# A depthwise conv as float32 products in column groups on TensorE, and the norms' sums and weight low parts off GpSimd

## The chip, the cores and the metric

One NeuronCore of a Trainium2 chip runs the whole program in one launch. The metric is the device time in microseconds (us) of the launch, median of several runs; smaller is better. TensorE multiplies a stationary tile (up to 128 x 128) with a moving one (up to 128 x 512) into PSUM; VectorE (DVE), ScalarE (ACT) and GpSimd (POOL) work elementwise; SyncE (SP) issues most DMAs.

## The reference

Two transformer blocks on 512 tokens of 1024 channels, float32. The first has a parallel mixer (conv branch and attention), cross attention to a memory of 256 tokens and a conv-gated feed-forward; the second has two layers of half-weighted SwiGLU around a pooling mixer and a latent attention (MLA). The change touches the mixer's conv branch and the norms:

```python
def rmsnorm(x, g):
    return x * lax.rsqrt(jnp.mean(x * x, axis=-1, keepdims=True) + EPS) * g

def parallel_mixer(h, ...):
    z = jnp.einsum("bsd,dc->bsc", h, w_in)           # 1024 -> 1792
    a_val, a_gate = z[..., :512], z[..., 512:1024]   # then q, k, v
    a = a_val * jax.nn.sigmoid(a_gate)
    a = dwconv_centred(a, conv_dw, conv_dw_b)        # 31 taps, each channel by itself
    a = jax.nn.silu(layernorm(a, conv_ln_g, conv_ln_b))
    ...
    return jnp.einsum("bsc,cd->bsd", jnp.concatenate([a, att], -1), w_out)

x = x + rmsnorm(parallel_mixer(rmsnorm(x, g1), ...), g2)     # block 1, and likewise
x = x + rmsnorm(memory_cross_attention(rmsnorm(x, g3), ...), g4)
x = x + rmsnorm(conv_gated_ffn(rmsnorm(x, g5), ...), g6)
```

## The kernel before

Activations lie transposed: 128 channels on the partitions, 512 tokens along the free dimension, so x is eight tiles `x0` to `x7`. Every float32 operand of a large product is split into two exact parts of a shorter format, hi (a cast on ScalarE) and lo (the rest, by a subtraction), and `mm3` (L165) makes three products of them: hi hi (L168), hi lo (L169) and lo hi (L170). Weights come through SP into `raw` (three buffers, 512 KB a unit, `fetch` L127); `cook` (L132) splits them, with the low part on VectorE or, for `wshare` of every four units, on GpSimd (`lo_on_pool`, L144). `linear` (L172) runs the products of one output tile after another into PSUM and calls an evacuation.

A tile framework places the instructions: it orders each engine's work by priority (place in the program) and by when operands and buffers are free by its own model, and sets the semaphores. On the chip each engine then runs its own list in order.

**Norms.** `sums` (L202) adds squares over the partitions: for each tile of squares four float32 products of 128 columns with a stationary tile of 32 columns of ones, one per block of 128 tokens, into PSUM partitions 0, 32, 64 and 96. The result is turned (`columns`), its reciprocal root found in eleven small VectorE operations (`newton`), and spread to rows by float32 products with the identity (`bcast_ps`). `gather` (L313) keeps the squares to two tiles: GpSimd adds all but the last. `pre` (L321) scales and splits x for the next stage and makes the squares; `post_collect` (L337) takes squares of a stage's output as it is evacuated; `settle` (L349), run by the next `pre`, multiplies the output's tiles by the rows (two on VectorE, six on GpSimd, L364) and adds them to x on VectorE (L369). Three stages end so: mixer, memory and conv_ffn. `warm` (L375) runs products that nobody reads while TensorE waits there.

**Mixer** (L561). `ORDER` runs the 14 output tiles of w_in: gate and value of four channel tiles, k, v and four q tiles. `ev_val` (L597) makes `at`, the gated channel tile, and queues `conv_taps` (L542): 31 taps, six of them on TensorE (`conv_pe`, three products each with diagonal matrices that GpSimd builds, L530), one on ScalarE, 24 on VectorE as multiply-and-add of a shifted `at` (L556). `step` interleaves them: six behind each w_in tile, 30 ahead of attention, eight a head. Attention runs eight heads, the scores one head ahead; two units of the memory's key and value projections (`mem_kv`, L464) follow each head. `conv_norm` (L737) runs in three steps at heads 3, 6 and 7. w_out takes attention's half first, then the conv's, into all eight PSUM buffers.

Of the kernel before, what the change touches and what calls it, by code (L numbers as in the profile page):

```python
# [26 lines left out]
# order of the taps' offsets: the even ones from the middle, then the odd ones  # L27
TAPS = sorted(range(-(KTAPS // 2), KTAPS // 2 + 1), key=lambda d: (d % 2, abs(d), d))
# [5 lines left out]
_VECS = [  # L34
    ("g_mix", 8), ("conv_w", 4 * KTAPS), ("conv_b", 4), ("cln_g", 4), ("cln_b", 4),
# [25 lines left out]
class Kern:  # L61
# [41 lines left out]
    # -- small access helpers --  # L103
# [7 lines left out]

    def t(self, tag="t", dt=F32, w=S, name="t"):
        return self.pools[tag].tile([P, w], dt, name=name, tag=tag)
# [43 lines left out]
    def load_tile(self, w, nt, nk):  # L157
        """Stationary tiles of output tile nt: list over k of (hi, lo) [P, P]."""
        res = []
        for k0 in range(0, nk, 8):  # L160
            n = min(8, nk - k0)
            res += self.tiles(self.load_unit(w[nt, :, k0 * P:(k0 + n) * P], n * P), n)
        return res

    def mm3(self, ps, w, x, start, stop):  # L165
        """ps += w.T @ x with w, x each given as exact (hi, lo) parts."""
        mm = self.nc.tensor.matmul
        mm(ps, w[0], x[0], start=start, stop=False)  # L168
        mm(ps, w[0], x[1], start=False, stop=False)  # L169
        self.mmi = mm(ps, w[1], x[0], start=False, stop=stop)  # L170
# [10 lines left out]
    # -- split an fp32 tile (SBUF or PSUM), optionally scaled per partition --  # L181
# [31 lines left out]
    def columns(self, sm, dim, eps=0.0, w=1):  # L213
        """sm / dim + eps in columns [P, block, w], in PSUM."""
# [8 lines left out]
    def newton(self, v, n):  # L223
        """rsqrt of v [P, n] on the vector engine."""
# [14 lines left out]
    def rstd(self, sqs, dim, nb=4):  # L239
        """rsqrt(mean + eps) in columns from squares [P, nb * P], summed over the list."""  # L240
        sm = self.sums([(self.c("ones"), sq) for sq in sqs], nb)
        v = self.columns(sm, dim, EPS)
        return self.newton(v.rearrange("p j r -> p (j r)"), nb)
# [24 lines left out]
    def bcast_ps(self, R, nb=4, w=1):  # L268
        """Columns to rows of all partitions (row r of w in its share of them), exact float32."""
# [14 lines left out]
    def expand(self, R, w, tag="t"):  # L284
        """Columns -> [32 * block + r, tokens], zero outside the block, as exact parts."""
# [13 lines left out]
    def spread(self, X, r, tag="mi"):  # L299
        """Row r of every block, on all partitions."""  # L300
# [6 lines left out]
    # -- residual stream --  # L307
# [5 lines left out]
    def gather(self, sqs, sq, last, w=S):  # L313
        """Sum of squares so far: at most two tiles, the last one kept apart."""
        if not sqs or last:
            return sqs + [sq]
        self.nc.gpsimd.tensor_tensor(out=sqs[0][:, :w], in0=sqs[0][:, :w], in1=sq[:, :w],  # L317
                                     op=ALU.add)
        return sqs

    def pre(self, gname, dve_squares=(), tag2="xs"):  # L321
        """Gain times x as exact parts, and the reciprocal rms in quadrant form."""
        xs, sqs = [], []
# [4 lines left out]
        for k in range(ND):  # L328
# [5 lines left out]
            sqs = self.gather(sqs, sq, k == ND - 1 or bool(dve_squares))  # L334
        return xs, self.rstd(sqs, D)

    def post_collect(self, gname, tag="xs"):  # L337
        """Evacuation of a stage's output that a norm follows; pre() of the next stage adds it."""
        st = self.pending = {"y": [], "sqs": []}

        def evac(nt, ps):
# [4 lines left out]
            st["sqs"] = self.gather(st["sqs"], sq, nt == ND - 1)  # L346
        return evac

    def settle(self):  # L349
        """Generator: adds the pending normed output to x, a tile a step."""  # L350
# [6 lines left out]
        R = self.rstd(st["sqs"], D)  # L357
# [15 lines left out]
    SETTLE = 2  # L373
# [32 lines left out]
    def rope(self, src, g, gs, cos, sin):  # L406
        """Rotary embedding along the partitions (pairs 16 apart), gains g, gs folded in."""
# [11 lines left out]
    def stack(self, src, r, tag, on_pool=False):  # L419
        """Exact parts of the 64 rows src[64 r:], one in each half of a tile."""  # L420
# [27 lines left out]
    def mem_prep(self):  # L448
        """Gain times memory as exact parts."""
# [14 lines left out]
    def mem_kv(self):  # L464
        """Generator: key and value projections of the memory, a weight unit a step."""
# [37 lines left out]
    NPE = 6  # L503
    PE_AT = 0
    CP_TAG = "pt"
    STEP_IN = 6
    KV_HEAD = 2
    STEP_PRE = 30
    STEP_HEAD = 8
    KT_TAG = "pr"  # L510
    PT_TAG = "t"
    CN_AT = (3, 6, 7)
    CN_AF = (0, 0, 1)
    ORDER = (0, 1, 8, 2, 3, 9, 4, 5, 10, 6, 7, 11, 12, 13)
    W_IN, W_KV, W_OUT, W_MEM = 4, 4, 0, 1

    def tap(self, n):
        """Output and input ranges of tap n."""
        d = TAPS[n]
        return (slice(0, S - d), slice(d, S)) if d >= 0 else (slice(-d, S), slice(0, S + d))  # L520

    def conv_pe(self, i, at):
        """The taps of channel tile i that run on PE, as products with diagonal matrices."""
        nc = self.nc
        ah, al = self.split(at, None, "cv", name="ah")
        ps = self.ps(self.CP_TAG, "cps")
        for n0 in range(0, self.NPE, 2):
            c = 2 * (i * KTAPS + n0)
            dg = self.t("pr", F32R, name="dg")
            nc.gpsimd.tensor_tensor(  # L530
                out=dg.rearrange("p (n t) -> p n t", n=4),
                in0=self.ident.unsqueeze(1).to_broadcast([P, 4, P]),
                in1=self.cws[:, c:c + 4].bitcast(F32).unsqueeze(2).to_broadcast([P, 4, P]),
                op=ALU.mult)
            for n in range(2):
                o, s = self.tap(n0 + n)
                hi, lo = dg[:, 2 * n * P:(2 * n + 1) * P], dg[:, (2 * n + 1) * P:(2 * n + 2) * P]
                self.mm3(ps[:, o], (hi, lo), (ah[:, s], al[:, s]), n0 + n == 0,
                         n0 + n == self.NPE - 1)
        return ps  # L540

    def conv_taps(self, i, at, acc):  # L542
        """Generator: the other taps of channel tile i, on DVE."""
        nc = self.nc
        w = lambda n: self.cwh[:, i * KTAPS + n:i * KTAPS + n + 1]
        first = KTAPS // 2
        o, sl = self.tap(first)
        nc.scalar.activation(acc[:, o], at[:, sl], AF.Identity, scale=w(first),  # L548
                             bias=self.v("conv_b", i))
        nc.gpsimd.tensor_copy(acc[:, :1], self.v("conv_b", i))  # L550
        ps = None
        for m, n in enumerate(n for n in range(self.NPE, KTAPS) if n != first):
            if m == self.PE_AT:
                ps = self.conv_pe(i, at)
            o, s = self.tap(n)
            nc.vector.scalar_tensor_tensor(out=acc[:, o], in0=at[:, s], scalar=w(n),  # L556
                                           in1=acc[:, o], op0=ALU.mult, op1=ALU.add)
            yield
        nc.vector.tensor_tensor(out=acc, in0=ps, in1=acc, op=ALU.add)

    def mixer(self):  # L561
        nc = self.nc
        a = self.a
        self.cwh = self.t("tb", name="cwh")[:, :4 * KTAPS]
        ws0 = {0: self.tiles(self.cook(self.raw0, UNIT, 4), 8)}
        xs, R1 = self.pre("g_mix", (1, 3, 5))
        nc.gpsimd.tensor_scalar(out=self.cwh, in0=self.v("conv_w", 0, 4 * KTAPS), scalar1=0.5,
                                scalar2=1.0, op0=ALU.mult, op1=ALU.mult)
        self.cws = self.t("tb", F32R, name="cws")[:, :8 * KTAPS]
# [823 lines left out]
```

## Time and profile before

| | us |
|---|---|
| median of three runs | 2589.59 (2588.21 to 2589.89) |
| span of the profiled execution | 2588.3 |
| TensorE products busy | 2496.1 (96%) |
| VectorE busy | 1385.5 (54%) |
| ScalarE busy | 919.1 (36%) |
| GpSimd busy | 521.8 (20%) |

The mixer lies at 0 to 321 us of the span, the memory's attention up to 460, the conv-gated feed-forward up to 842; the rest is block 2. A matmul's busy time includes its way through the array, so neighbours overlap, and the spacing of starts is the better measure of what one costs. The profile's clock column is the share of TensorE's full clock that was granted, a mean over a stretch; it has two levels, 2.4 GHz (1.00) and 1.2 GHz (0.50). Each float32 product shows as two instructions.

### The profile page before, as it was taken

What the parts mean: (1) busy time and instruction counts of PE and PEld (TensorE: products, weight loads), DVE (VectorE), ACT (ScalarE), POOL (GpSimd) and SP (SyncE); (2) the same over time, 40 slices, a digit from 0 to 9 for tenths busy, and PEclk for the clock granted to TensorE, in tenths of its full rate; (3) what the DMA queues carried; (4) which work ended last, traced back from release to release, by engine and by line L of the source; (5) the groups of instructions that cost most, each with busy time, mean ns of one, the idle gap of its engine ahead of it and who ended that gap; (6) DMA issues with size and microseconds to landing.
All of it is one profiled execution on the core that took longest, in us unless ns stands there. A gap on an engine that the chain in (4) does not pass through costs nothing.

```text
span 2588.3 us, 29365 instructions
## 1 busy us (share of the span) xinstructions
PE 2496.1 (96%) x11668; PEld 2037.2 (79%) x11668; DVE 1385.5 (54%) x1877; ACT 919.1 (36%) x1332; POOL 521.8 (20%) x417
## 2 busy tenths in 40 slices
PE   7879989899999899999999999999999999999999
PEld 6667768688888688888888888888887778888887
DVE  7997563686632645533655543555433576555522
ACT  3336534354422333322422322323222455422221
POOL 4575232311100311101211100111000144111100
PEclk9889999999999999999999999999999999999999
DMA  4211211133333222234232333223332210333232
GB/s 163 66 67 49 90 57 58 64 98 98 96 95 97 69 94 96 95 98 132 74 98 98 97 98 96 97 95 95 98 98 88 78 62 19 104 98 97 92 107 79
DMA packets 68201, 229.80 MB, mean 89 GB/s; under 512 B 7456, under 2 KB 9632, under 8 KB 68064
## 3 DMA queue, kind: packets, MB, share of 16 engines
q1 hardware_dynamic: 66688, 225.35, 27.1%
q0 software_dynamic: 1232, 2.36, 0.3%
q8 instruction: 91, 1.49, 0.2%
q14 instruction: 46, 0.38, 0.0%
q10 hardware_dynamic: 144, 0.23, 0.0%
HBM read 225.80 MB, written 2.10 MB: 88 GB/s over the span
## 4 chain that ended last, share of the span: by engine, by line
PE 86%; DVE 4%; ACT 1%; issue 0%; ACTq 0%
PE ps L169 26%; PE ps L168 26%; PE ps L170 26%; DVE x L369 1%; DVE xl L190 1%; PE wo L168 1%; PE wo L169 1%; PE wo L170 1%; PE pt L124 1%; PE po L169 0%; PE bc L274 0%; PE po L168 0%; PE po L170 0%; PE sc L168 0%; DVE wlo L140 0%
## 5 line engine op out<-in xcount | busy, mean ns | idle before, releaser
L138 ACT CAST whi<-raw 128x1024 fp32r<-128x1024 f32 (+2 forms) x432 | 440.5, 1021 | 1217.7 <-PE ps L169 767.5
L140 DVE TENSOR_TENSOR wlo<-raw,whi 128x1024 fp32r<-128x1024 f32 (+2 forms) x400 | 559.3, 1400 | 492.6 <-ACT whi L138 487.5
L169 PE MATMUL ps<-xl,whi 128*128 128x512 f32 x2008 | 789.8, 394 | 18.6 <-DVE xl L190 18.5
L168 PE MATMUL ps<-xh,whi 128*128 128x512 f32 x2008 | 784.9, 393 | 15.0 <-ACT xh L189 14.7
L170 PE MATMUL ps<-xh,wlo 128*128 128x512 f32 x2008 | 786.6, 392 | 0.0
L169 PEld LDWEIGHTS ps<-xl,whi 128*128 128x128 f32 x2008 | 380.5, 189 | 104.6 <-DVE xl L190 25.0
L168 PEld LDWEIGHTS ps<-xh,whi 128*128 128x128 f32 x2008 | 379.7, 189 | 97.3 <-ACT xh L189 16.2
L170 PEld LDWEIGHTS ps<-xh,wlo 128*128 128x128 f32 x2008 | 380.7, 190 | 79.8 <-issue 0.9
L168 PE MATMUL ps<-ah,whi 128*128 128x512 f32 x880 | 342.3, 389 | 0.0
L169 PE MATMUL ps<-al,whi 128*128 128x512 f32 x880 | 342.3, 389 | 0.0
L170 PE MATMUL ps<-ah,wlo 128*128 128x512 f32 x880 | 342.3, 389 | 0.0
L877 DVE TENSOR_TENSOR g<-ps,bct 128x512 f32<-128x512 f32 x176 | 120.6, 691 | 389.9 <-PE ps L170 382.8
L882 POOL TENSOR_TENSOR g<-g 128x512 f32<-128x512 f32 x88 | 119.0, 1353 | 856.5 <-ACT whi L138 457.6
L317 POOL TENSOR_TENSOR sq<-sq 128x512 f32<-128x512 f32 x72 | 112.7, 1566 | 535.8 <-ACT sq L310 533.9
L170 PEld LDWEIGHTS ps<-ah,wlo 128*128 128x128 f32 x880 | 165.2, 188 | 34.4
L169 PEld LDWEIGHTS ps<-al,whi 128*128 128x128 f32 x880 | 165.2, 188 | 34.2
L168 PEld LDWEIGHTS ps<-ah,whi 128*128 128x128 f32 x880 | 165.2, 188 | 34.2
L556 DVE SCALAR_TENSOR_TENSOR acc<-at,cwh,acc 128x502 f32<-128x502 f32 (+12 forms) x96 | 114.1, 1201 | 1.0 <-ACT acc L548 0.5
L140 POOL TENSOR_TENSOR wlo<-raw,whi 128x1024 fp32r<-128x1024 f32 x32 | 81.3, 2542 | 71.4 <-ACT whi L138 71.2
L185 ACT CAST ah<-g 128x512 fp32r<-128x512 f32 x88 | 54.7, 622 | 112.8 <-POOL g L882 112.8
L387 DVE SCALAR_TENSOR_TENSOR x<-ps,x 128x512 f32<-128x512 f32 x40 | 27.5, 691 | 84.5 <-PE ps L170 84.4
L858 POOL TENSOR_TENSOR c<-c 128x512 f32<-128x512 f32 x22 | 29.7, 1348 | 208.3 <-DVE c L845 178.5
(298 smaller groups left out, 2594.8 us busy)
## 6 DMA issues: line engine op xcount, KB each, us to landing
raw<-in_wgu SPq DMA_DIRECT2D x176, 512.0 KB, 3.5
raw<-in_wd SPq DMA_DIRECT2D x64, 512.0 KB, 3.5
raw<-in_w_up SPq DMA_DIRECT2D x44, 512.0 KB, 3.5
raw<-in_wd SPq DMA_DIRECT2D x32, 384.0 KB, 3.1
raw<-in_w_down SPq DMA_DIRECT2D x16, 512.0 KB, 3.5
raw<-in_w_in SPq DMA_DIRECT2D x14, 512.0 KB, 4.0
raw<-in_mla_w_in SPq DMA_DIRECT2D x9, 512.0 KB, 3.5
raw<-in_mla_w_q SPq DMA_DIRECT2D x12, 384.0 KB, 3.0
```

The lines of the kernel that those rows point to most:

```text
L138: self.nc.scalar.copy(hi[:, s], raw[:, s])
L140: eng.tensor_tensor(out=lo[:, s], in0=raw[:, s], in1=hi[:, s].bitcast(F32), op=ALU.subtract)
L168: mm(ps, w[0], x[0], start=start, stop=False)
L169: mm(ps, w[0], x[1], start=False, stop=False)
L170: self.mmi = mm(ps, w[1], x[0], start=False, stop=stop)
L185: nc.scalar.copy(hi, src)
L317: self.nc.gpsimd.tensor_tensor(out=sqs[0][:, :w], in0=sqs[0][:, :w], in1=sq[:, :w], op=ALU.add)
L387: self.nc.vector.scalar_tensor_tensor(out=self.x[nt], in0=ps, scalar=scale, in1=self.x[nt], op0=ALU.mult, op1=ALU.add)
L556: nc.vector.scalar_tensor_tensor(out=acc[:, o], in0=at[:, s], scalar=w(n), in1=acc[:, o], op0=ALU.mult, op1=ALU.add)
L858: nc.gpsimd.tensor_tensor(out=c, in0=c, in1=st["g"], op=ALU.mult)
L877: nc.vector.tensor_tensor(out=g, in0=ps, in1=rb, op=ALU.mult)
L882: nc.gpsimd.tensor_tensor(out=g, in0=g, in1=st["g"], op=ALU.mult)
```

## The change

The conv's 31 taps move to TensorE whole. `ev_val` writes the gated tile into a buffer with zeroed borders (`xp`, 544 wide). `conv` copies its 32-channel strips, by DMAs on SP, into four tiles `cx`: strip c four times, shifted by 0, 8, 16 and 24 columns. One product of such a tile, moved by m columns, with a stationary tile of 32 columns that holds the weights of taps m, 8 + m, 16 + m and 24 + m on diagonals, adds four taps for 32 channels; the four strips go to four groups of 32 PSUM partitions. Eight steps m of four products make a channel tile, in float32 without splitting. The weights come in that layout from the host, one unit a channel tile. ScalarE evacuates with the factor one half and the bias. The convs follow heads 0, 0, 1 and 2, the conv's norm heads 4, 5 and 6.

The low parts of w_in and of the memory's keys and values move from GpSimd to VectorE (`W_IN`, `W_KV` 4 to 0). `gather` goes: each tile of squares is summed by its own four products as soon as it is there (`pile`, one PSUM buffer per norm). `settle` multiplies all eight tiles on VectorE. Comments and docstrings are taken out.

```diff
-    def conv_pe(self, i, at):
-    def conv_taps(self, i, at, acc):
...
+    def conv_in(self):
+        xp = self.t("cv", w=self.WIDE["cv"], name="cp")
+        self.nc.gpsimd.memset(xp[:, :HALO], 0.0)
+        self.nc.gpsimd.memset(xp[:, HALO + S:], 0.0)
+        return xp
+
+    def conv(self, i, xp):
+        nc = self.nc
+        wd = self.fetch(self.a["conv_d"][i], UNIT)
+        W = S + STEPS - 1
+        X = []
+        for c in range(4):
+            t = self.t("xs", w=S + STEPS, name="cx")
+            for j in range(SHIFTS):
+                nc.sync.dma_start(out=t[32 * j:32 * j + 32, :W],
+                                  in_=xp[32 * c:32 * c + 32, STEPS * j:STEPS * j + W])
+            X.append(t)
         ps = self.ps(self.CP_TAG, "cps")
+        for m in range(STEPS):
+            for c in range(4):
+                o = (4 * m + c) * 32
+                nc.tensor.matmul(ps[32 * c:32 * c + 32, :], wd[:, o:o + 32], X[c][:, m:m + S],
+                                 start=m == 0, stop=m == STEPS - 1)
+        acc = self.t("cv", name="acc")
+        nc.scalar.activation(acc, ps, AF.Identity, scale=0.5, bias=self.v("conv_b", i))
+        return acc
...
-    W_IN, W_KV, W_OUT, W_MEM = 4, 4, 0, 1
+    W_IN, W_KV, W_OUT, W_MEM = 0, 0, 0, 1
...
-            with self.tc.issue_after(self.mxi.ins):
-                step(self.STEP_HEAD if n < self.CN_AT[0] else 1000)
+            for i in range(4):
+                if n == self.CONV_AT[i]:
+                    accs.append(self.conv(i, xps[i]))
...
+    def pile(self, n, tag="mi"):
+        st = {"i": 0}
+        def add(sq):
+            if not st["i"]:
+                st["ps"] = self.ps(tag, "sum")
+            st["i"] += 1
+            st["sm"] = self.sums([(self.c("ones"), sq)], ps=st["ps"], start=st["i"] == 1,
+                                 stop=st["i"] == n)
+            return st["sm"]
+        return add
...
-            sqs = self.gather(sqs, sq, k == ND - 1 or bool(dve_squares))
-        return xs, self.rstd(sqs, D)
+            sm = add(sq)
+        return xs, self.rsqrt(sm, D)
...
-            st["sqs"] = self.gather(st["sqs"], sq, nt == ND - 1)
+            st["sm"] = add(sq)
...
-        for k in range(self.SETTLE, ND):
-            nc.gpsimd.tensor_tensor(out=st["y"][k], in0=st["y"][k], in1=rs, op=ALU.mult)
         for k in range(ND):
             y = st["y"][k]
-            if k < self.SETTLE:
-                nc.vector.tensor_tensor(out=y, in0=y, in1=rb if k == 0 else rs, op=ALU.mult)
+            nc.vector.tensor_tensor(out=y, in0=y, in1=rb if k == 0 else rs, op=ALU.mult)
             nc.vector.tensor_tensor(out=self.x[k], in0=self.x[k], in1=y, op=ALU.add)
```

## Rows read from the trace of the kernel before

**Rows 1.** Page, part 1: busy us (share of the span) xinstructions of each engine.
```profile
PE 2496.1 (96%) x11668; PEld 2037.2 (79%) x11668; DVE 1385.5 (54%) x1877; ACT 919.1 (36%) x1332; POOL 521.8 (20%) x417
```
**Rows 2.** Stretches: start:end, length, busy of each engine (instructions), clock, DMA share, GB/s.
```profile
0.00:40.00 40.00, 31.93 (x189) 24.91 (x190) 23.02 (x44) 19.44 (x30) 17.94 (x17) 1.00 0.57 200
40.00:138.00 98.00, 81.84 (x376) 63.86 (x375) 96.87 (x124) 28.34 (x45) 52.47 (x34) 0.91 0.23 76
138.00:186.00 48.00, 32.20 (x200) 30.24 (x199) 46.25 (x66) 16.75 (x27) 35.72 (x21) 0.79 0.20 66
186.00:321.00 135.00, 125.70 (x614) 99.28 (x612) 90.60 (x175) 79.70 (x146) 58.83 (x48) 0.99 0.21 71
...
467.20:481.00 13.80, 6.79 (x21) 4.11 (x19) 13.79 (x10) 5.40 (x9) 13.59 (x9) 0.67 0.00 0
```
**Rows 3.** TensorE's groups by shape, 0 to 321 us: count, busy, mean ns, idle before.
```profile
L168 PE MATMUL ps<-xh,whi 128*128 128x512 f32 x112 | 47.3, 422 | 7.4 <-ACT xh L189 7.4
...
L168 PE MATMUL ps<-mh,whi 128*128 128x256 f32 x64 | 21.0, 329 | 14.2 <-DVE mk L479 7.7 <-DVE nb L398 4.3 <-DVE sh L413 2.2
...
L124 PE MATMUL pt<-con,p 128*128 128x128 f32 x128 | 20.2, 273 | 0.0
L688 PE MATMUL sc<-kh,st 128*128 128x512 f32 x32 | 14.2, 445 | 2.2 <-ACT p L400 2.2
...
L168 PE MATMUL po<-pth,vh 128*128 128x512 f32 x32 | 13.5, 423 | 0.3 <-ACT pth L185 0.3
...
L168 PE MATMUL ps<-whi,mh 128*128 128x512 f32 x32 | 12.8, 421 | 2.6 <-DVE mk L479 2.2 <-ACT whi L138 0.4
...
L168 PE MATMUL wo<-mixh,whi 128*128 128x512 f32 x32 | 12.2, 403 | 1.3 <-ACT bct L281 0.7 <-ACT mixh L185 0.7
...
L745 PE MATMUL mean<-tot,con 128*128 128x512 f32 x2 | 1.1, 644 | 0.7 <-DVE tot L743 0.7
```
**Rows 4.** Page, part 5: costliest groups, busy and mean ns, idle before and releaser.
```profile
L140 DVE TENSOR_TENSOR wlo<-raw,whi 128x1024 fp32r<-128x1024 f32 (+2 forms) x400 | 559.3, 1400 | 492.6 <-ACT whi L138 487.5
...
L556 DVE SCALAR_TENSOR_TENSOR acc<-at,cwh,acc 128x502 f32<-128x502 f32 (+12 forms) x96 | 114.1, 1201 | 1.0 <-ACT acc L548 0.5
L140 POOL TENSOR_TENSOR wlo<-raw,whi 128x1024 fp32r<-128x1024 f32 x32 | 81.3, 2542 | 71.4 <-ACT whi L138 71.2
```
**Rows 5.** TensorE in order of time: start us, us, engine, line, operation, tiles.
```profile
15.12 1.74 PE L208 MATMUL sum<-sq,con 128*32 128x128 f32 x56
...
312.04 0.39 PE L170 MATMUL wo<-ch,wlo 128*128 128x512 f32 x1
312.27 0.39 PE L168 MATMUL wo<-ch,whi 128*128 128x512 f32 x1
...
1969.86 0.39 PE L170 MATMUL ps<-ah,wlo 128*128 128x512 f32 x1
1970.18 0.43 PE L208 MATMUL sum<-sq,con 128*32 128x128 f32 x8
1970.53 0.50 PE L168 MATMUL ps<-xh,whi 128*128 128x512 f32 x1
1970.87 0.39 PE L169 MATMUL ps<-xl,whi 128*128 128x512 f32 x1
```
**Rows 6.** In order of time behind the memory's output: GpSimd, VectorE, TensorE.
```profile
467.25 9.64 POOL L364 TENSOR_TENSOR y<-y,rs 128x512 f32<-128x512 f32 x6 [8.96 <-ACT rs L362]
475.69 1.76 DVE L190 SCALAR_TENSOR_TENSOR xl<-x,vec,xh 128x512 fp32r<-128x512 f32 x1
477.50 0.80 PE L169 MATMUL ps<-xl,whi 128*128 128x512 f32 x1 [4.61 <-DVE xl L190]
...
485.83 0.74 DVE L190 SCALAR_TENSOR_TENSOR xl<-x,vec,xh 128x512 fp32r<-128x512 f32 x1
```
**Rows 7.** SP's queue in order of time, the loads of x.
```profile
1.19 5.02 SPq L94 DMA_DIRECT2D x<-in_xT  x8
```

More of the change, by code (lines that the diff above doesn't have):

```diff
@@ L26 @@
 KTAPS = 31
-TAPS = sorted(range(-(KTAPS // 2), KTAPS // 2 + 1), key=lambda d: (d % 2, abs(d), d))
+HALO = KTAPS // 2
+SHIFTS, STEPS = 4, 8
 UNIT = 1024
@@ L110, in c @@
         return self.con[:, o:o + w]
+    WIDE = {"xs": S + STEPS, "cv": S + SHIFTS * STEPS}
     def t(self, tag="t", dt=F32, w=S, name="t"):
-        return self.pools[tag].tile([P, w], dt, name=name, tag=tag)
+        return self.pools[tag].tile([P, self.WIDE.get(tag, S)], dt, name=name, tag=tag)[:, :w]
     def ps(self, tag="ps", name="ps"):
@@ L239, in rstd @@
     def rstd(self, sqs, dim, nb=4):
-        sm = self.sums([(self.c("ones"), sq) for sq in sqs], nb)
-        v = self.columns(sm, dim, EPS)
-        return self.newton(v.rearrange("p j r -> p (j r)"), nb)
+        return self.rsqrt(self.sums([(self.c("ones"), sq) for sq in sqs], nb), dim, nb)
     @staticmethod
@@ L311, in square, with rsqrt @@
         return sq
[L313 to L319, printed above, removed]
+    def pile(self, n, tag="mi"):
[8 more added lines that the diff above has]
+        return add
+    def rsqrt(self, sm, dim, nb=4):
+        v = self.columns(sm, dim, EPS)
+        return self.newton(v.rearrange("p j r -> p (j r)"), nb)
     def pre(self, gname, dve_squares=(), tag2="xs"):
-        xs, sqs = [], []
+        xs, add = [], self.pile(ND)
         settle = self.settle()
@@ L333, in pre @@
                 sq = self.square(self.x[k])
[L334 to L335 removed]
+            sm = add(sq)
+        return xs, self.rsqrt(sm, D)
     def post_collect(self, gname, tag="xs"):
[L339 removed]
+        st = self.pending = {"y": []}
+        add = self.pile(ND)
         def evac(nt, ps):
@@ L522, in conv_pe @@
-    def conv_pe(self, i, at):
-        nc = self.nc
-        ah, al = self.split(at, None, "cv", name="ah")
-        ps = self.ps(self.CP_TAG, "cps")
[L527 to L540, printed above, removed]
@@ L542, in conv_taps @@
-    def conv_taps(self, i, at, acc):
[L544 to L559, printed above, removed]
+    W_IN, W_KV, W_OUT, W_MEM = 0, 0, 0, 1
@@ L584, in ev_gate @@
             st["g"] = g
-        convs = []
-        accs = []
-        def step(n):
-            while n and convs:
-                try:
-                    next(convs[0])
-                    n -= 1
-                except StopIteration:
-                    convs.pop(0)
+        xps, accs = [], []
         def ev_val(nt, ps):
-            i = nt // 2
-            at = self.t("cv", name="at")
-            acc0 = self.t("cv", name="acc0")
+            at = self.t(name="at")
             nc.vector.tensor_tensor(out=at, in0=ps, in1=rb, op=ALU.mult)
-            nc.vector.scalar_tensor_tensor(out=at, in0=st["g"], scalar=1.0, in1=at, op0=ALU.add,
-                                           op1=ALU.mult)
-            accs.append(acc0)
-            convs.append(self.conv_taps(i, at, acc0))
+            xp = self.conv_in()
+            nc.vector.scalar_tensor_tensor(out=xp[:, HALO:HALO + S], in0=st["g"], scalar=1.0,
+                                           in1=at, op0=ALU.add, op1=ALU.mult)
+            xps.append(xp)
         ks, vh = [], []
@@ L667, in mixer @@
                 self.mem_prep()
-            step(self.STEP_IN)
         fcol = self.inner_rstd(qsum[:, :P], 64, R1, 8, post=64.0 ** -0.5)
         self.wshare = self.W_KV
-        after = self.last.ins
         self.kv = self.mem_kv()
-        with self.tc.issue_after(after):
-            step(self.STEP_PRE)
         mix = []
@@ L713, in mixer @@
             attend(n)
-            with self.tc.issue_after(self.mxi.ins):
-                step(self.STEP_HEAD if n < self.CN_AT[0] else 1000)
+            for i in range(4):
+                if n == self.CONV_AT[i]:
+                    accs.append(self.conv(i, xps[i]))
             for _ in range(self.KV_HEAD):
                 next(self.kv)
-            for i in range(3):
-                if n == self.CN_AT[i]:
-                    with self.tc.issue_after((self.loi if self.CN_AF[i] else self.mxi).ins):
-                        next(cn)
+            if n in self.CN_AT:
+                next(cn)
         self.wshare = self.W_OUT
@@ L1032, in mla @@
         self.linear(w, [8], xs, ev_kpe, ("sc",))
-        Rkv = self.inner_rstd(self.sums([(ones, q) for q in sqs["kv"]]), 256, R)
+        Rkv = self.inner_rstd(self.sums([(ones, q) for q in sqs]), 256, R)
         bkv = self.bcast(Rkv, "pr")
         self.linear(w, range(6), xs, ev_cq, tags)
-        Rq = self.inner_rstd(self.sums([(ones, q) for q in sqs["q"]]), 768, R)
+        Rq = self.inner_rstd(sm["q"], 768, R)
         kraw = []
@@ L1334, in host_arrays @@
         .reshape(2, 4, P, UNIT))
+    w = f("conv_dw")[0].reshape(KTAPS, 4, 4, 32)
+    cd = np.zeros((4, SHIFTS, 32, STEPS, 4, 32), np.float32)
+    for d in range(KTAPS):
+        for c in range(32):
+            cd[:, d // STEPS, c, d % STEPS, :, c] = w[d, :, :, c]
+    out["conv_d"] = cd.reshape(4, P, UNIT)
     out["rope1"] = _axial_rope()
```

35 lines of the change are left out of this document (8 added, 27 removed).

## The prediction, made blind

> **What bounds the kernel now.** I read the engines' shares first: TensorE is busy 96% of the span [rows 1], so whatever gains must either fill the other 4%, raise the granted clock, or remove products; whatever adds products pays for them. Then busy time by stretch, to find where the 4% lies. From 361 us on, TensorE is nearly full but for the norms between stages. In the mixer, 0 to 321 us, it is idle for 8.1, 16.2, 15.8 and 9.3 us in four stretches, 49 us together, and VectorE is busy 97 of 98 and 46 of 48 us in the middle two, with TensorE's clock at 0.91 and 0.79 [rows 2]: VectorE sets the pace there.
>
> How much is there to win? I counted the mixer's products and priced each at its spacing when nothing waits. Neighbours of 512 columns start 0.227 us apart [rows 5]. Each row of [rows 3] named L168 has two partners, L169 and L170, of the same count. So: w_in 336 x 0.227 = 76; memory keys 192 x 0.12 (half the columns) = 23; memory values 96, and the values of attention 96, 22 each; scores 64 = 15; 128 transposes of a quarter width, about 0.11, = 14; w_out 192 = 44; the six conv taps on TensorE, 4 x 6 x 3 = 72, = 16. That is 232, and about 9 for sums, broadcasts and transposes of norms: 241 us of work in 321 us. 80 us are lost: the 49 of idle time, some 20 at half clock (a mean of 0.79 over 48 us between levels of 1.2 and 2.4 GHz is 20 us at the lower, so 10 lost; 0.91 over 98 us loses 9), the rest where engines hand over.
>
> **The change, part by part.**
>
> *Conv off VectorE.* 96 taps of 114 us go [rows 4], with the four splits and four final sums beside them (about 8). In exchange 28 low parts (all of GpSimd's 32 but the memory stage's four) move from GpSimd to VectorE: 28 x 1.4 = 39 us [rows 4]. VectorE then has about 60 of the 143 us it works between 40 and 186, and it no longer binds. GpSimd loses 28 x 2.54 = 71 us, so VectorE operations that read two SBUF tiles are slowed less often [rows 6].
>
> *Conv on TensorE.* Gone: 72 products, 16.3 us. New: per channel tile 8 steps of four float32 products of 512 columns, each into 32 output rows: 128 in all. The trace has this shape at 128 columns, in the norms' sums: 56 instructions (28 products, two instructions each) take 1.74 us, so four products in 0.21 to 0.25 us [rows 5]. A full-width float32 product of 512 columns takes 1.1 us alone in two instructions [rows 3], about 0.85 in a stream if the 0.21 of 128 columns is scaled by four. So the four groups run abreast, and one step of four costs what one full-width product costs: 32 x 0.85 = 27.3 us. Other end: not abreast at 512 columns, 128 x 0.85 = 109 us. I take 27, since the near row has the same form and separate moving data for each group.
>
> The Trainium skill (TensorE: Matmul & The Clock Gate, Part 3, measured speedup) gives three column groups a speedup of 2.38, not 3; the row above shows no such shortfall. At that efficiency the conv would be 34 us, 7 more, an estimate from that page which my range covers.
>
> *Entering and leaving the column groups.* A lone group of four sums between 512-column products delays them by more than its own 0.21: starts at 1969.86, 1970.53, 1970.87 with the group between [rows 5] mean 0.67 + 0.34 instead of 2 x 0.227, so 0.56 us per lone group; 0.34 of it is the change of shape. For the conv that is 4 x 0.34 if each tile runs unbroken, 32 x 0.34 = 11 us if every step is split off; I take 5.
>
> *The copies.* Each conv tile issues 16 SBUF-to-SBUF copies and one weight load on SP, 68 in all. SP issues a load every 0.63 us [rows 7]: 43 us of SP. Behind them stand the weight fetches of the memory's keys and values, three buffers deep, so 3 x 2.9 us (24 products of 0.12) of cover against 10.7 us per tile. The bounds are 0 (issued while w_in or attention's products run) and about 20 us (two tiles back to back, less the cover); I take 5.
>
> *The mixer's sum.* Work: 241 - 16 + 27 + 3 (six more sums behind w_out and two in the conv's norm) = 255. Losses: 12 at the start, until x has landed; 5 for shapes; 5 for copies; in attention, whose stretch from 186 us already has its other engines free of taps for most of its length, 9 us of idle time in 135 [rows 2], and now some 130 us of TensorE work there, about 13; 2 at w_out. Together 292 against 321: -29 (from -14 to -43).
>
> *Norms between stages* (three of them). After the reciprocal root is there, GpSimd multiplies six tiles in 9.64 us, and each VectorE addition or low part meanwhile takes 1.76 us instead of 0.74; the first low part lands so late that TensorE waits until 477.50 [rows 6]. Between 467.2 and 481 us it runs 21 products, 4.8 us of work in 13.8, at clock 0.67 [rows 2]. Afterwards VectorE does three operations of about 0.7 per tile: 2.1 us a tile, the first low part done after about 3.6 us instead of 10.2 (475.69 + 1.76 - 467.2), the last after about 16.6. TensorE has three output tiles begun, 9 x 0.227 = 2.04 us per tile, so it nearly keeps up. Loss after: about 4 for the start, 0 to 5 for waits, and six more groups of sums (0.22 to 0.56 each, 1.3 to 3.4, partly in the waits). Against 11 now: -3 each, and -4 behind the mixer, where two output tiles at a time can be begun: -10 (from 0 to -18).
>
> *Sums on TensorE elsewhere.* A norm now has eight groups instead of two. Behind w_mem_o and w_down they come one at a time between products that have no gap: 12 x 0.56 = 6.7 us. In the MLA's latent norm 4 x 0.56 = 2.2. In the five norms without a normed output to add, seven squares can be summed in one burst (7 x 0.21 + 0.34) and one alone (0.56), 2.4 instead of 1.1: +1.3 each, 6.5; all alone, +17. The GpSimd additions that go were under TensorE's work and give nothing. Together +15 (10 to 26).
>
> Total: -29 - 10 + 15 = -24. The profiled span of 2588.3 stands 1.3 under the median, 2589.6, and I take the difference from the median: 2565.
>
> **Rivals.**
> 1. *The mixer fills up.* Taps gone, memory products and conv fill every wait of attention, as w_in's products do in the first 40 us, where the 8 us of idle time are the wait for x [rows 2]; the mixer takes 275 and norms gain 15: about 2543. For it: the clock then stays up. Against: the chain from scores to transposes stays.
> 2. *SP's queue or the attention chain becomes the bound.* The copies cost 20 instead of 5, or the chain of softmax through GpSimd stalls: 2580 to 2588, no change in the limit.
> 3. *Column groups don't run abreast at 512 columns.* Place: the conv's 128 products. Price: up to 82 us over the 27. It ends above the old time once a step of four costs more than 0.85 + 24/32 = 1.6 us instead of 0.85; not abreast it gives 2565 + 82 = 2647, slower. Against it: the burst of 56.
> 4. *Changes of shape cost everywhere.* All 54 added groups outside the mixer's waits lone and each conv step split: +6 in the mixer, +11 in the norms: about 2582.
>
> **How the numbers follow.** Forecast 0.5; rival 1 0.17; rival 2 0.18; rival 3 0.06; rival 4 0.09. Predicted time 2565. The range leaves out rival 3 and the ends: 2537 to 2590. 0.2% is 5 us, about what a measurement of this kernel can tell from no change. Faster than 2584.4: the forecast, rivals 1 and 4, and most of rival 2, 0.85; slower than 2594.8: rival 3 and a tail of 2, 0.08; within: 0.07.
>
> **What would show it.** The mixer should end between 280 and 305 us with no taps on VectorE, which is then idle a third of 40 to 186 us, and clock near 1. The conv's groups should show eight instructions every 0.85 us; a spacing of 3.4 us would be rival 3. In the norms behind a stage, low parts of 0.74 us and the first within 4 us of the reciprocal root's rows. Gaps of TensorE ended by a weight's high part, while SP issues copies, would be rival 2. Sums one at a time in w_down, starts 0.67 us apart around each, would confirm the price of a lone group; the forecast is wrong if these are not gaps in a full stream but lie in idle time.

## The result, and the profile after

The median went from 2588.9 us (2587.63 to 2589.89) to 2625.61 us (2624.71 to 2626.3), a ratio of 1.0141 (95% interval 1.0127 to 1.0156): 1.4% slower, where a gain of 0.9% was forecast. Times are medians of several executions; one of the ten of `before_shift` below took 5138.96 us, for a cause that is not known. The profiled execution of after spans 2623.9 us. Page, part 1 of after, beside [rows 1]:

```profile
PE 2570.8 (98%) x12428; PEld 2036.5 (78%) x12428; DVE 1263.5 (48%) x1819; ACT 916.2 (35%) x1327; POOL 285.3 (11%) x289
```

The relief is there: VectorE lost 122 us of work and GpSimd 237. TensorE is busy 75 us longer. The mixer's stretches of after, beside [rows 2], have the same columns (the mixer ends at 305.1 us instead of 321.1):

```profile
0.00:40.00 40.00, 32.52 (x193) 25.15 (x194) 23.23 (x47) 18.13 (x27) 4.27 (x19) 1.00 0.55 199
40.00:138.00 98.00, 90.53 (x503) 65.86 (x505) 57.39 (x125) 41.83 (x75) 29.45 (x27) 0.97 0.34 106
138.00:186.00 48.00, 48.00 (x337) 30.37 (x333) 23.89 (x48) 22.05 (x41) 9.27 (x11) 1.00 0.40 126
186.00:305.00 119.00, 111.11 (x608) 85.08 (x600) 61.38 (x110) 62.38 (x104) 14.29 (x17) 0.99 0.25 85
```

In the two middle stretches VectorE is free for 65 of 146 us (98 - 57.39 + 48 - 23.89), TensorE waits for 7.5 us there instead of 32, and its clock is near the upper level (0.97 and 1.00 instead of 0.91 and 0.79). So the mixer did nearly what it should, and the time was lost elsewhere. By the starts of the stages (worked out from the trace: the first `warm` product of a norm, or the last write to x of a stage), in us:

```
stage       mixer  memory  conv_ffn  ffn1_0  pool+ffn2_0  ffn1_1    MLA  ffn2_1
before      321.1   139.1     381.0   381.2        386.6   361.3  253.7   360.3
after       305.1   139.8     390.5   387.0        396.6   370.5  259.6   370.7
```

Every stage behind the mixer is longer, also ffn1_1 and ffn2_1, in which the change only adds a few sums. The reason stands in a stretch where TensorE never waits and where nothing is new: the same 200 us of a feed-forward, first of before, then of after. The figure in the first brackets, the number of TensorE's products behind its busy time, is the one to read:

```profile
1700.00:1900.00 200.00, 200.00 (x884) 165.62 (x883) 92.55 (x87) 58.64 (x72) 21.77 (x17) 1.00 0.31 97
```

```profile
1700.00:1900.00 200.00, 200.00 (x865) 162.09 (x865) 94.01 (x88) 58.67 (x72) 22.18 (x16) 1.00 0.29 93
```

Clock 1.00 and 100% busy in both, and after starts 19 products fewer: 200/884 is 0.226 us a product, 200/865 is 0.231. TensorE's timeline of after, where [rows 5] has neighbours 0.227 apart (start, duration, line and operation):

```profile
1499.49 0.39 PE L173 MATMUL ps<-ah,wlo 128*128 128x512 f32 x1
...
1500.65 0.39 PE L172 MATMUL ps<-al,whi 128*128 128x512 f32 x1
1500.88 0.40 PE L173 MATMUL ps<-ah,wlo 128*128 128x512 f32 x1
```

Six spacings in 1.39 us, 0.232 each, with the duration of one as it was. Over the whole span, the 9,660 or so neighbours of 512 columns that stand without a gap have a mean spacing of 227.11 ns before and 231.88 after: 4.8 ns x 9,660 is 46 us. That is the loss, and it lies in products that the change doesn't touch.

What the change does touch behind their backs is where their operands lie. `xs` tiles become 520 columns wide, `cv` tiles 544, and every buffer allocated behind them moves. Worked out from the allocation, the start of each buffer in its partition, modulo 256 bytes:

```
           weights (hi, lo)   xs                 cv         m, q, t
before     32                 32                 32         32
after      32                 all 8 steps of 32  32 or 160  160
```

Before, the moving and the stationary tile of every large product started at the same place modulo 256 bytes. After, few pairs do: 2 of the 16 `xs` buffers and 5 of the 9 `cv` buffers, and no `m`, `q` or `t` buffer, start where the weights do.

### The profile page after: what moved, and what is told of

The parts are those of the page before. It is cut to its first block, busy times and chain, and to the rows that moved or that the text cites. A ratio compares the mean times of both kernels' runs of the same rounds, so it can differ in the third digit from the quotient of the medians.

```text
span 2623.9 us, 30744 instructions
## 1 busy us (share of the span) xinstructions
PE 2570.8 (98%) x12428; PEld 2036.5 (78%) x12428; DVE 1263.5 (48%) x1819; ACT 916.2 (35%) x1327; POOL 285.3 (11%) x289
## 4 chain that ended last, share of the span: by engine, by line
PE 95%; DVE 3%; ACT 1%; issue 0%; DMA 0%; ACTq 0%; DVEq 0%
PE ps L171 28%; PE ps L172 28%; PE ps L173 28%; PE cps L543 1%; PE sum L211 1%; PE pt L127 1%; PE wo L171 1%; PE po L172 1%; PE wo L173 1%; PE wo L172 1%; DVE y L376 1%; PE po L173 1%; PE po L171 1%; PE bc L275 0%; PE sc L171 0%
## 5 line engine op out<-in xcount | busy, mean ns | idle before, releaser
L143 DVE TENSOR_TENSOR wlo<-raw,whi 128x1024 fp32r<-128x1024 f32 (+2 forms) x428 | 594.4, 1390 | 545.7 <-ACT whi L141 534.0
L171 PE MATMUL ps<-xh,whi 128*128 128x512 f32 x2008 | 796.7, 397 | 20.1 <-ACT xh L192 20.1
L190 DVE TENSOR_TENSOR al<-g,ah 128x512 fp32r<-128x512 f32 x88 | 59.8, 680 | 15.0 <-ACT ah L188 15.0
L407 ACT ACTIVATE p<-sc,nb,f 128x512 f32<-128x512 f32 (+3 forms) x80 | 53.7, 676 | 35.8 <-DVE nb L405 33.6
L190 DVE TENSOR_TENSOR ptl<-pt,pth 128x512 fp32r<-128x512 f32 (+1 forms) x72 | 42.7, 596 | 42.1 <-ACT pth L188 42.0
L803 DVE TENSOR_TENSOR u<-ps,bct 128x512 f32<-128x512 f32 x44 | 30.2, 690 | 65.8 <-PE ps L173 65.1
```

The costliest lines, as they stand in the source:

```text
L143: eng.tensor_tensor(out=lo[:, s], in0=raw[:, s], in1=hi[:, s].bitcast(F32), op=ALU.subtract)
L190: self.loi = eng.tensor_tensor(out=lo, in0=src, in1=hi.bitcast(F32), op=ALU.subtract)
L407: nc.scalar.activation(p[:, :w], ps[:, :w], AF.Exp, bias=nb, scale=f, accum_out=l)
L803: nc.vector.tensor_tensor(out=u, in0=ps, in1=rb, op=ALU.mult)
```

## The experiments

**The widths alone, and a shift of everything.** Two kernels from before, with nothing else of the change:

```diff
-        return self.pools[tag].tile([P, w], dt, name=name, tag=tag)
+        w = {"xs": 520, "cv": 544}.get(tag, S)
+        return self.pools[tag].tile([P, w], dt, name=name, tag=tag)[:, :S]
```

> The kernel before, with nothing changed but the width of two kinds of buffers (xs 512 to 520 columns, cv 512 to 544), as the change has them; every instruction and every operand's shape stays. Theory L (layout: products of 512 columns start 231.7 ns apart in the changed kernel and 226.7 in the one before, because its moving and stationary tiles no longer start at the same offset within 2048 bytes): spacing near 231.7 ns in all stages, some 9,300 products x 5 ns, so about 2635 us. Rival I (the added instructions, changes of shape or added load on TensorE slow it everywhere): spacing 226.7, 2589 us.

```diff
+        self.gap = self.cp.tile([P, 384], F32, name="gap")
```

> The kernel before, with an unused table of 384 columns behind the constants, so that all weight and activation tiles move together by 1536 bytes and keep their offsets against each other (32 instead of 544 within 2048 bytes, the weights' place in the changed kernel). Theory L-relative (what counts is how moving and stationary tiles lie against each other): spacing 226.7 ns, 2589 us. Theory L-absolute (what counts is where the tiles lie): spacing near 231.7 ns, about 2635 us. Rival I: 2589 us.

Measured: `before_wide` 2633.29 us, ratio 1.0174 (1.0159 to 1.0189); `before_shift` 2588.33 us, ratio 0.9999 (0.9989 to 1.0009). Spacing 231.83 and 227.09 ns. The stretch of 1700 to 1900 us of each, first `before_wide`:

```profile
1700.00:1900.00 200.00, 200.00 (x867) 162.42 (x866) 95.80 (x88) 57.89 (x72) 22.53 (x17) 1.00 0.30 95
```

```profile
1700.00:1900.00 200.00, 200.00 (x884) 165.62 (x883) 92.15 (x87) 58.66 (x72) 21.38 (x17) 1.00 0.32 97
```

867 products as in after, and 884 as in before. So the widths by themselves cost 44.5 us, more than the whole change; TensorE's 11668 instructions are those of before, in the same order. Moving all tiles together costs nothing. That alone doesn't separate the place of a tile from how two tiles stand to each other: 1536 bytes are 6 x 256, so modulo 256 bytes nothing has moved. The map that follows separates them.

**A map of the offsets.** A kernel of products alone, the block left out: 24 products of the split format by 512 columns for each pair of offsets (`m` of the moving and `b` of the stationary tile, in columns of 4 bytes).

```diff
+    for m, b in configs():
...
+        for i in range(n):
+            k, r = (i // 3) % 4, i % 3
+            w = W[1 if r == 2 else 0][:, b + k * P:b + (k + 1) * P]
+            x = X[1 if r == 1 else 0][:, m:m + S]
+            nc.tensor.matmul(ps, w, x, start=i == 0, stop=i == n - 1)
```

> No part of the block is computed: 136 groups of 24 products of 512 columns, as the three products of the split parts, with the moving tiles moved by 0 to 2016 bytes in steps of 32, then the stationary ones by 0 to 992, then both together. Theory L-relative: 226.7 ns wherever both moved alike, and up to 240 ns in a pattern of the difference elsewhere. Theory L-absolute: a pattern when both move together, too. Rival I: 226.7 ns in every group.

Measured, mean spacing of starts (worked out from the trace), moving offset modulo 256 bytes against a stationary tile at 0:

```
offset, bytes      0    32     64     96    128    160    192    224
spacing, ns    226.65 233.3 228.75 233.95  233.3 234.35 233.35 233.35
```

It repeats every 256 bytes over the 2 KB tried (227.15 at the later multiples). A stationary tile that is moved instead gives 233.3 at 32 bytes, 228.75 at 192 (which is -64) and 226.65 at 256. Both moved alike, in steps of 32 bytes, give 227.70 throughout: the first eight spacings of such a group, behind the step from the group before, are uneven (224 to 236 ns), and the others are 226 to 227. So the difference of the two starts counts, modulo 256 bytes, and not the place; it costs between 0 and 7.7 ns of 226.65, 3.4% at most. The mean of the eight values is 232.1, and the two kernels whose `xs` tiles stand at all eight offsets have 231.88 and 231.83.

**One offset in the whole kernel.** Before, with 64 unused bytes between the weights' buffers and the activations':

```diff
+        gap = E(tc.tile_pool(name="gap", bufs=1))
+        self.gap = gap.tile([P, 16], F32, name="gap")
```

> The kernel before with 64 unused bytes between the weight buffers and the activation buffers: every moving tile then starts 64 bytes later against the stationary tiles within 256 bytes, and nothing else changes. Theory L-relative with the probe's table (228.75 ns at a difference of 64 bytes, 226.65 at 0, 233.3 at most others): 9,300 products x 2.1 ns = 20 us, 2608 us. Rival T (any difference costs the 5 ns of the changed kernel): 2635. Rival W (only the mixed offsets of wider buffers cost, a common one doesn't): 2589.

Measured: 2609.19 us, ratio 1.0077 (1.0060 to 1.0094), spacing 229.10 ns. The map's step at 64 bytes, 2.1 ns x 9,660 = 20 us, is what it costs (20 more than before). The same stretch, between the two others:

```profile
1700.00:1900.00 200.00, 200.00 (x875) 164.14 (x874) 93.88 (x88) 58.64 (x72) 21.43 (x16) 1.00 0.30 95
```

**The change with its tiles put back in line.** Everything of the change is kept, but eight `xs` buffers are 512 columns wide again, eight others (`xw`) 576, which is a multiple of 256 bytes; the gated tile goes into a plain `cv` tile, and the borders are zeroed in `cx`:

```diff
-("xs", 16), ("cv", 9)
+("xs", 8), ("xw", 8), ("cv", 9)
-    WIDE = {"xs": S + STEPS, "cv": S + SHIFTS * STEPS}
+    WIDE = {"xw": S + 64}
...
-            t = self.t("xs", w=S + STEPS, name="cx")
+            t = self.t("xw", w=S + STEPS, name="cx")
+            nc.gpsimd.memset(t[:, :HALO], 0.0)
+            nc.gpsimd.memset(t[:, W - HALO - 1:W], 0.0)
```

> The changed kernel with its instructions for TensorE as they are, but buffers laid so that moving and stationary tiles start alike within 256 bytes: the xs buffers are parted in 8 of 512 and 8 of 576 columns, the conv's shifted tiles take the wide ones, and their borders are zeroed instead of those of the source (32 small memsets on GpSimd). Theory L-relative: spacing 226.7 ns, about 47 us less than the changed kernel, 2579 us, faster than before. The blind forecast's sum without the layout: 2565. Rival I (what the change adds to TensorE slows it beside the layout): over 2600.

Measured: 2575.1 us, ratio 0.9946 (0.9931 to 0.9960), spacing 227.10 ns. The same change is now a gain, 50.5 us under after. Of these, 4.8 ns x 9,660 = 46 us are the spacing; the other 4 go with the copies, the borders and the planner's order of instructions, which move too. The mixer ends at 296.4 us, 24.7 sooner than before. Its middle stretches, with a clock of 0.95 and 1.00, and the stretch of the feed-forward with 884 products again:

```profile
40.00:138.00 98.00, 90.48 (x527) 64.58 (x528) 52.31 (x115) 40.03 (x70) 30.48 (x49) 0.95 0.35 105
138.00:186.00 48.00, 46.39 (x331) 29.16 (x324) 22.81 (x45) 20.37 (x36) 9.75 (x18) 1.00 0.43 136
...
1700.00:1900.00 200.00, 200.00 (x884) 165.59 (x883) 86.65 (x84) 58.39 (x71) 16.13 (x12) 1.00 0.30 96
```

**The sums on TensorE, undone where they bring nothing.** From `aligned`, GpSimd adds the squares again in the norms that don't follow a stage with a normed output, in w_mem_o, w_down and the latent norm:

```diff
-        xs, add = [], self.pile(ND)
+        xs, add = [], self.pile(ND) if bool(dve_squares) or self.pending is not None else self.heap(ND)
...
-        add = self.pile(ND)
+        add = self.heap(ND)
...
-        sqs, add, sm = [], self.pile(6, "po"), {}
+        sqs, add, sm = [], self.heap(6), {}
```

> The aligned kernel with the norms' squares added on GpSimd again, as before the change, wherever TensorE has no wait to fill: behind w_out, w_mem_o and w_down, in the five norms without a normed output to add, and in the latent norm. The three norms behind a stage keep their eight groups on TensorE. Forecast's term (sums on TensorE elsewhere cost 15 us, 10 to 26): 15 less than the aligned kernel, about 2564. Rival: the added groups lie in waits, no difference.

Measured: 2560.43 us, ratio 0.9887 (0.9872 to 0.9902), 14.7 less than `aligned`: the forecast's term was 15. (1.3 of it lies in the mixer, behind w_out, whose six sums the forecast had counted in the mixer's work.) Its price is in the trace of after, a group of sums between two products of w_down, as in [rows 5]:

```profile
729.75 0.40 PE L171 MATMUL ps<-ah,whi 128*128 128x512 f32 x1
730.08 0.43 PE L211 MATMUL sum<-sq,con 128*32 128x128 f32 x8
730.44 0.51 PE L172 MATMUL ps<-al,whi 128*128 128x512 f32 x1
730.78 0.39 PE L173 MATMUL ps<-ah,wlo 128*128 128x512 f32 x1
```

Spacings of 0.69 and 0.34 instead of two of 0.232: 0.57 us for the group (forecast: 0.56).

**The norms between stages, undone.** From `aligned`, `settle` with six multiplications on GpSimd and its squares added there, as before:

```diff
-        xs, add = [], self.pile(ND)
+        xs, add = [], self.pile(ND) if bool(dve_squares) or self.pending is None else self.heap(ND)
...
+        for k in range(2, ND):
+            nc.gpsimd.tensor_tensor(out=st["y"][k], in0=st["y"][k], in1=rs, op=ALU.mult)
         for k in range(ND):
             y = st["y"][k]
-            nc.vector.tensor_tensor(out=y, in0=y, in1=rb if k == 0 else rs, op=ALU.mult)
+            if k < 2:
+                nc.vector.tensor_tensor(out=y, in0=y, in1=rb if k == 0 else rs, op=ALU.mult)
```

> The aligned kernel with the three norms behind a stage as before the change: six of eight multiplications and the squares' additions there on GpSimd, all else as in the aligned kernel. Forecast's term (10 us gained there by leaving GpSimd, 0 to 18): 10 more than the aligned kernel, about 2589. Rival (the eight groups of sums eat what the faster VectorE gives): no difference.

Measured: 2578.13 us, ratio 0.9957 (0.9942 to 0.9972), 3.0 more than `aligned`, not 10. So small a difference is hardly clear of the noise: the two intervals overlap, and the four times of each lie within 2573.64 to 2578.04 and 2577.87 to 2579.43. By the stages of the two profiles, the three behind these norms take 5 us more together (memory +4.1, conv_ffn -0.9, ffn1_0 +2.0), and the MLA, in which nothing was changed, 2.5 less. VectorE's timeline of the norm behind memory in `aligned` shows why it isn't 10 (start, duration, line, operation, count):

```profile
440.48 0.69 DVE L376 TENSOR_TENSOR y<-y,bc 128x512 f32<-128x512 f32 x1 [1.93 <-ACT rs L373]
441.09 4.29 DVE L376 TENSOR_TENSOR y<-y,rs 128x512 f32<-128x512 f32 x7
445.30 4.90 DVE L377 TENSOR_TENSOR x<-x,y 128x512 f32<-128x512 f32 x8
450.12 5.38 DVE L193 SCALAR_TENSOR_TENSOR xl<-x,vec,xh 128x512 fp32r<-128x512 f32 x8
```

All eight multiplications come first, then eight additions, then eight low parts. Each takes 0.6 to 0.7 us, as the forecast had it, but the first low part is done 10.4 us after the rows (450.12 + 0.74 - 440.48), as late as before (10.2, [rows 6]). TensorE's clock in the 13.8 us from the rows is 0.70, and it is busy 8.82 of them.

**Who issues the copies.** From `aligned_gather`, the 64 copies of the strips on GpSimd's queue, or on ScalarE's:

```diff
-                nc.sync.dma_start(out=t[32 * j:32 * j + 32, o:e],
+                nc.gpsimd.dma_start(out=t[32 * j:32 * j + 32, o:e],
```

> The kernel aligned_gather with the conv's 64 shifted copies issued from GpSimd's queue instead of SP's. Forecast's rival 2 (copies on SP hold back the weights of the memory's projections; TensorE waits 7 us at one place between 100 and 140 us at a mean clock of 0.87): that wait shrinks, 5 to 10 us less, about 2553. Rival A (the wait is the softmax chain's own): no difference, 2560. Rival B (copies issued from GpSimd take longer to start and the conv comes later): 2560 to 2570.

```diff
-                nc.sync.dma_start(out=t[32 * j:32 * j + 32, o:e],
+                nc.scalar.dma_start(out=t[32 * j:32 * j + 32, o:e],
```

> The same with the copies on ScalarE's queue, which also casts weights and makes the softmax's exponentials. If SP's queue is what holds TensorE: 2553 as well, less what 64 issues of about 0.6 us take from ScalarE if they hold its casts (up to 38 us of its time, half of it idle before): 2550 to 2575. Rival A: 2560 or more.

Measured: 2573.64 us (ratio 0.9942, 0.9926 to 0.9959) on GpSimd's, 2560.0 us (0.9891, 0.9876 to 0.9905) on ScalarE's. Taking the copies off SP brings no gain: 2560.0 against 2560.43. That alone would not clear SP's queue, since ScalarE could lose what SP gives; its expectation allowed for that. The waits say more. On SP in after, the first two tiles' copies stand at (start, duration, queue, line, count)

```profile
96.63 20.54 SPq L536 DMA_DIRECT2D cx<-cp  x32
```

0.64 us each, and no weight unit is late because of them: TensorE's waits from 40 to 305 us of after (in all, times, longest) are led by softmax, and none of 0.4 us or more is for a weight:

```profile
PE sc L652 <- ACT p L407: 6.8, 3, 6.3
PE po L172 <- DVE ptl L190: 4.8, 5, 3.1
```

In `aligned_gather` there is one, rival 2's sign on a small scale: at 149.8 us TensorE waits for a weight of the memory's keys that SP issued at 144.8, behind 16 copies.

```profile
PE ps L171 <- ACT whi L141: 1.6, 1, 1.6
```

With the copies on ScalarE's queue this wait is gone and the time is the same, so what SP's queue holds back is 1.6 us at one place.

GpSimd's queue is another matter, and slower than all three expectations. In `aligned_poolq` the copies stand between its multiplications of the softmax and of the rotary embedding, 0.5 us each, and TensorE waits longer for the same tile (11.3 us in all instead of 7.5); its clock from 40 to 138 us is 0.88 instead of 0.95, and the mixer ends at 307.8 us instead of 295.1:

```profile
PE sc L671 <- ACT p L425: 11.3, 5, 7.2
```

**Which products lose.** A second kernel of products alone, the block left out:

```diff
+    for kind, n, m in (("r", 512, 128), ("r", 256, 128), ("r", 128, 128), ("r", 512, 64),
+                       ("r", 512, 32), ("f", 512, 128), ("b", 512, 128)):
+        for o in (0, 8, 16, 32):
+            res.append((kind, n, m, [(o, 0)] * 24))
```

> No part of the block is computed: groups of 24 products with the moving tile 0, 32, 64 and 128 bytes off its stationary one, for products of 512, 256 and 128 columns, for stationary tiles of 64 and 32 columns, for float32 and bfloat16; then stationary tiles that alternate between two or three places, with the moving tile placed like its own stationary one, like the next one's or like the one before's. Theory N (a moving tile is read while the next stationary tile is loaded, and the two reads get in each other's way unless they run alike within 256 bytes): 226.7 ns where the moving tile lies like the next stationary one, 228 to 234 where it lies like its own; with 64 or 32 stationary columns the loss shrinks to a half or a quarter. Theory O (a product's own two operands must lie alike): the other way round, and no less for fewer columns.

Measured, mean spacing in ns by the offset of the moving tile (stationary at 0):

```
offset, bytes                          0      32      64     128
split format, 512 columns         226.65  233.35  228.75  232.55
split format, 256 columns         119.70  117.75  117.75  118.65
split format, 128 columns         111.65  111.65  111.75  111.65
split, 64 stationary columns      230.20  231.20  228.30  229.35
split, 32 stationary columns      231.65  231.95  231.70  230.70
float32, an instruction            429.2   429.2   429.2   429.2
bf16                              215.85  215.85  215.85  215.85
```

Only products of the split format with 512 moving and 128 stationary columns lose clearly; with 64 or 32 stationary columns they start every 228 to 232 ns at every offset, in line or not. With stationary tiles that alternate between 0 and 32 bytes, a moving tile in line with its own stationary tile starts after 233.45 ns, one in line with the next after 236.25; with 0 and 128 bytes it is 228.50 and 229.95, and with three places (0, 32 and 64) 230.85 and 232.85. Neither of the two explanations put against each other above gives these numbers. What in the chip makes the offset count stays open.

**VectorE's order, forced.** From `aligned_gather`: the multiplication of tile k has to follow the low part of tile k - 2.

```diff
+            if k < 2:
+                nc.vector.tensor_tensor(out=y, in0=y, in1=rb if k == 0 else rs, op=ALU.mult)
+            else:
+                with self.tc.issue_after(los[k - 2].ins):
+                    nc.vector.tensor_tensor(out=y, in0=y, in1=rs, op=ALU.mult)
```

> This is aligned_gather with one thing forced: in the norms that follow a stage, VectorE may multiply output tile k by the rows only once the low part of tile k-2 is done, so that its list goes two multiplications, two additions, then low part, multiplication, addition by turns, instead of eight multiplications, eight additions, eight low parts. Theory (the change gained 3 us there instead of 10 because of that order): the first low part is done 4 to 5 us after the rows instead of 10.4, TensorE starts its products behind the norm some 5 us sooner and loses 2 to 3 us less in each of three norms: 2550 to 2555 us against 2560.4. Rival (each low part then waits for ScalarE's high part, which waits for the addition, so that the list stands still between tiles and the last low part, 15 us after the rows now, comes later): the first low part is early, the last at 18 us or more, and the time is 2558 to 2566 us.

Measured: 2549.44 us, ratio 0.9848 (0.9832 to 0.9864), 11.0 less than `aligned_gather`: the best of all, 1.5% under before. VectorE behind memory now:

```profile
435.53 0.69 DVE L397 TENSOR_TENSOR y<-y,bc 128x512 f32<-128x512 f32 x1 [1.93 <-ACT rs L392]
436.13 0.69 DVE L397 TENSOR_TENSOR y<-y,rs 128x512 f32<-128x512 f32 x1
436.74 1.29 DVE L401 TENSOR_TENSOR x<-x,y 128x512 f32<-128x512 f32 x2
438.21 0.75 DVE L193 SCALAR_TENSOR_TENSOR xl<-x,vec,xh 128x512 fp32r<-128x512 f32 x1 [0.19 <-ACT xh L192]
...
451.38 0.75 DVE L193 SCALAR_TENSOR_TENSOR xl<-x,vec,xh 128x512 fp32r<-128x512 f32 x1 [0.38 <-ACT xh L192]
```

The first low part is done 3.4 us after the rows and the last 16.6: the prediction's own 3.6 and 16.6. The last one comes later than in `aligned` (15.0), and that costs nothing, since TensorE is at work meanwhile. The 13.8 us from the rows, first of `aligned_gather`, then of `aligned_order`:

```profile
437.52:451.32 13.80, 8.82 (x51) 4.92 (x50) 13.80 (x23) 8.26 (x15) 0.00 (x0) 0.69 0.00 0
```

```profile
435.53:449.33 13.80, 13.04 (x80) 8.25 (x78) 13.24 (x21) 7.14 (x12) 0.00 (x0) 1.00 0.01 1
```

TensorE runs 80 instructions instead of 51, at clock 1.00 instead of 0.69: it hardly stops behind the norm (busy 13.04 of 13.8 us), and the clock does not fall there. Memory, conv_ffn and ffn1_0, the three stages behind such norms, are 2.2, 5.6 and 4.6 us shorter.

## Why the prediction was wrong

The mechanism of the change was judged nearly right; what decides the sign isn't in the sum. By terms, in us, with what the runs give for each:

```
term                              forecast   measured   from
mixer                                  -29      -24.7   aligned against before
sums on TensorE elsewhere              +15      +14.7   aligned against aligned_gather
norms between stages                   -10       -3.0   aligned against aligned_pool
where the operands lie                 none     +50.5   after against aligned
```

The four terms add up to +37.5, and the change measured +36.7. Without the last one they give -13 instead of the forecast's -24: 4 are missing in the mixer, 7 in the norms.

- *The step that failed* is the pricing of everything that the change leaves alone: "neighbours of 512 columns start 0.227 us apart" was taken as a price of the product. It is a price of the product at the place its operands have before. The widths of 520 and 544 stood in the diff, and I read them as capacity only. The trace of before shows one offset alone, so it could not give the size; but a change of buffer widths under 9,660 products is a resource that the trace doesn't show, and it got no bound. None of the four rivals names it; the one slower rival, column groups not abreast, missed as well. (By the spacing, 46 of the 50.5 are the layout; the widths alone in `before_wide` cost 44.5.)
- *The mixer* is 4 us short of the forecast and within its range, once the tiles are in line; in after itself it is 16 us shorter than before. VectorE is free and the clock up, as forecast.
- *Conv in column groups* was right. TensorE in after, for the third channel tile:

```profile
151.09 3.64 PE L543 MATMUL cps<-cx,raw 128*32 128x512 f32 x30
154.66 0.50 PE L171 MATMUL po<-pth,vh 128*128 128x512 f32 x1
155.09 1.05 PE L543 MATMUL cps<-cx,raw 128*32 128x512 f32 x4
```

  By their starts (worked out from the trace), four instructions begin within 21 ns of each other and the next four 430 ns behind them, so a step of eight takes 0.86 us (forecast 0.85). A full-width float32 product is 2 x 0.429 = 0.858 us in the second map, so four products in four groups cost what one costs. The Trainium skill (TensorE: Matmul & The Clock Gate, Part 3, measured speedup) has 2.38 for three groups; here four give 4 x 0.858 / 0.86 = 4.0, and the measurement decides. The attention's products break the runs up, as the second line shows.
- *The copies* cost SP 0.64 us each (forecast 0.63) and held back one weight for 1.6 us in `aligned_gather`; the 5 us charged for them are not seen when the queue is relieved of them. Their upper bound of about 20 was a slip: two tiles less the cover are 2 x 10.7 - 8.7 = 12.7.
- *Sums elsewhere* were right in size and place: a full stream, 0.57 us a lone group.
- *Norms between stages:* the durations were right, the order was not. I had put the instructions tile by tile, because the code is written so; the framework placed them by kind, and the first low part came no sooner than before. The list is the planner's, and the trace of before, in which GpSimd spaced the tiles, could not show it. With the order forced, the norms bring 3.0 + 11.0, about 14 us, 4 more than the forecast; the 3.0 is the uncertain part.

## What to carry to other kernels

When a change alters the width or number of buffers, look where every buffer behind them comes to lie, and keep the operands of long streams of split-format products equal modulo 256 bytes: here widths of 512 and 576 float32 columns, multiples of 64, were enough. If a stretch that a change doesn't touch gets slower, count its products per stretch of full clock before looking for waits. And the order in which a planner puts an engine's list is a part of the price: what helps is the first result early, not the last one soon.

## What the runs showed of the hardware

A product of the split format, 512 by 128 columns, starts every 226.65 ns when its moving and stationary tile start at the same place modulo 256 bytes, and every 228.75 to 234.35 ns otherwise; with widths of 520 and 544 that was 44.5 us of 2589. Products of float32 (429.2 ns an instruction), of bf16 (215.85) and of 256 or 128 columns show no such loss. Why is open. Four column groups of 32 output rows run abreast in float32 without a loss at 512 columns: 0.86 us for four products against 0.858 for one of full width. A VectorE operation of 512 columns that takes 0.74 us alone takes 1.76 beside GpSimd ([rows 6]); behind the memory in `aligned`, with nothing on GpSimd, all of them take 0.6 to 0.75.
